# A hybrid decoder step: fewer VectorE instructions for GELU, gate and the samples' convolution, and the S5 recurrence in blocks

## The chip, the cores and the metric

The kernel runs on one core of one Trainium2 chip. The metric is the device time of one execution in microseconds, as the median of several runs. TensorE is called PE here, VectorE DVE, ScalarE ACT, GpSimd POOL, and SP is the engine that issues the DMAs.

## The reference

One inference step of two layers runs over a prompt of 16 + 512 tokens and over 8 samples of 8 tokens, with shared weights. Only layer 0 is touched by the change. It projects the input (width 2048) into five groups of 1024 columns and computes two branches:

```
h   = u_a * sigmoid(g_a)                                   # GLU
y_a = silu(LayerNorm(depthwise_conv31([state, h]) + b)) @ pw
x_t = a * x_(t-1) + B u_t      (64 groups, 64 complex states each)
y   = Re(C x) + D u_b
vg  = gelu(y) @ glu_w + glu_b;   y_b = v * sigmoid(gt)
mix = [y_a * silu(z_a), y_b * silu(z_b)];   out = mix @ w_out
x   = LayerNorm(ALPHA * x + out)
```

The samples start from given states (30 earlier rows of `h`, and the S5 state), the prompt from zeros. The states after the last token are outputs too.

## The kernel before

Activations lie channels on partitions, tokens along the free axis: 528 prompt columns and 8 x 8 sample columns, 592 in all (NP, NT). A projection is a list of jobs, one for each stripe of 128 output channels. A job takes the weights in pieces of four 128 x 128 blocks. Each piece is loaded by SP (`wraw`), rounded by ACT into `wh`, and DVE writes the remainder `wl = wraw - wh`. PE then runs 24 matmuls for it: three products (`wh` with both halves of the input, `wl` with the upper half), two column spans, four blocks. There are three `wraw`, two `wh` and two `wl` buffers, so a new `wh` waits for PE to finish an older piece.

Layer 0 (`layer0`) runs as several threads: loads, splits, matmuls, results of jobs, S5 tables, S5 application, convolution, normalisation. A planner (`Weave.run`) merges them at build time. It keeps an assumed clock for each engine, adds an assumed cost for each instruction (`cost`), and of the instructions that could start next takes the thread with the lowest number (splits first, convolution near the end). What comes out is one fixed order on each engine. On the chip each engine works through that order, and an instruction that waits holds all behind it. All these instructions carry the line of the planner's emission, L321, so they are told apart by tile names.

The parts in question: `glu_gate` and `glu` are two jobs for a stripe; the first turns `g_a` into a sigmoid in the tile `sg`, the second multiplies it into `hh`, a row of 862 columns (30 zeros, the prompt, then 8 samples of 30 + 8). `conv_taps` sums 31 shifted products of `hh` in the accumulator `taps`, which lies in PSUM: for each tap one DVE instruction on the prompt and one on the samples. The jobs function gives out stripe j's gate only when the taps of stripe j - 2 are all planned (`S.taps`), and gives out other jobs (inputs, `gates`) until then.

`s5_chain` runs on POOL, once for each half of the groups. It carries the chunk state through 66 chunks of 8 tokens in `s5xv`: product with the 2 x 2 form of a^8, sum of its two terms, sum into the next chunk. `s5_tables` and `s5_inject_tables` build matrices on POOL for PE, `s5_out` copies states to `s5xpad` on POOL, gathers PE's results in `s5y` and applies the GELU with `s5q`. `s5_setup` computes the powers of a once on DVE, at the start.

After the convolution the normalisation (`norms`) makes the input of the pointwise jobs (`pw`), `cbh` and `cbl`. The GELU results are loaded back and are the input of the `w_glu` jobs. Then `out_proj` follows, and layer 1, with code of their own.

Of the kernel before, what the change touches and what calls it, by code (L numbers as in the profile page):

```python
# [11 lines left out]
F32 = mybir.dt.float32  # L12
F32R = mybir.dt.float32r
I32 = mybir.dt.int32
# [561 lines left out]
def s5_setup(K, pool, S):  # L576
# [13 lines left out]
    dt, mag, th = t_("dt"), t_("mag"), t_("th")  # L590
    tmp = t_("ean"), t_("ear"), t_("eae", sh, I32)
# [5 lines left out]
    n = t_("n")  # L597
# [8 lines left out]
    sn, cs = t_("sn"), t_("cs")  # L606
# [11 lines left out]
    t1, t2 = t_("t1"), t_("t2")  # L618
# [38 lines left out]
    S.a8 = t_("a8", [128, 2, 2, 32])  # L657
# [3 lines left out]
    yield V.tensor_copy(S.a8[:, 0, 1], S.npi[:, :, 8])  # L661
    S.cr, S.ci = t_("cr", b3), t_("ci", b3)
# [124 lines left out]
def s5_out(K, pool, S, j, tables, u, yb, ahead):  # L787
# [43 lines left out]
def conv_taps(K, P, j, h, c, acc):  # L831


    cw = P["convw"][:, 31 * j:31 * j + 31]
    b8 = lambda z: z.rearrange("p (b t) -> p b t", b=8)
    hs = b8(h[:, 558:])
    for k in range(31):
        for sl, cut, src in ((slice(0, NP), lambda z: z, h[:, k:k + NP]), (slice(NP, NT), b8, hs[:, :, k:k + 8])):
            o = cut((c if k == 30 else acc)[:, sl])
            if k == 0:  # L840
                yield K.V.tensor_scalar(o, src, cw[:, 0:1], P["convb"][:, j:j + 1], op0=OP.mult, op1=OP.add)
            else:
                yield K.V.scalar_tensor_tensor(o, src, cw[:, k:k + 1], cut(acc[:, sl]), op0=OP.mult, op1=OP.add)


def layer0(K, O):
# [3 lines left out]
    with mk("l0") as p0:  # L850
# [3 lines left out]
        with banks(K, sps=2), mk("ln0") as pl, mk("cc", 8) as pc, mk("zs") as pz, ExitStack() as mid, \  # L854
# [50 lines left out]

            def glu_gate(j):
# [1416 lines left out]
```

## Time and profile before

| | us |
|---|---|
| median of 3 runs | 2764.46 |
| lowest and highest | 2763.84, 2769.56 |
| the profiled execution | 2762.25 |
| its span, first to last instruction | 2760.5 |
| PE, DVE, ACT, POOL busy in it | 2624.8, 1692.7, 1065.4, 963.7 |

An engine's busy time is the time in which it ran at least one instruction. The table of stretches gives this time for pieces of the span, with the clock that TensorE was granted there as a share of full speed. The list of waits gives the idle time of an engine just before an instruction, put down to whichever releaser came last. Busy time that lies beside a busier engine costs nothing by itself.

### The profile page before, as it was taken

How to read it: one execution, taken by the hardware profiler on the slowest of the kernel's cores; microseconds unless marked ns; L12 is line 12 of the kernel's file. 1: busy time of each engine (PE TensorE's matmuls, PEld its weight loads, DVE VectorE, ACT ScalarE, POOL GpSimd, SP SyncE). 2: the span in 40 equal slices, each digit the busy share in tenths (PEclk: the TensorE clock that was granted, in tenths of full speed). 3: DMA queues.
4: the chain of work that ended last, by engine and by line, in shares of the span. 5: the costliest groups of instructions: out<-in, count | busy, mean ns of one | idle time of the engine just before them, and what ended most of it. 6: DMA issues, size and time to landing. Idle time of an engine off the chain costs nothing. (4 is left out here: it accounts for less than half of the span.)

```text
span 2760.5 us, 49648 instructions
## 1 busy us (share of the span) xinstructions
PE 2624.8 (95%) x18848; PEld 2530.0 (92%) x18848; DVE 1692.7 (61%) x3282; ACT 1065.4 (39%) x2291; POOL 963.7 (35%) x1776
## 2 busy tenths in 40 slices
PE   8998899899999998999999999999999999999996
PEld 8998899899999998998888998998999989898996
DVE  7679798873443357666767667667563444446337
ACT  4322322252222234544545445455333334334223
POOL 1885677510002223244244253245200212212533
PEclk9999999999999999999999999999999999999998
DMA  6333343444333333212222222222333423425333
GB/s 197 94 98 90 99 103 87 98 129 135 114 101 111 104 117 113 85 61 79 71 67 77 75 77 69 65 78 68 100 105 88 138 91 124 140 86 169 115 110 103
DMA packets 202095, 278.33 MB, mean 101 GB/s; under 512 B 66808, under 2 KB 86008, under 8 KB 201856
## 3 DMA queue, kind: packets, MB, share of 16 engines
q1 hardware_dynamic: 199552, 270.30, 32.6%
q10 hardware_dynamic: 2304, 4.85, 0.5%
q8 instruction: 148, 2.42, 0.4%
q14 instruction: 91, 0.75, 0.1%
HBM read 232.54 MB, written 42.53 MB: 100 GB/s over the span
## 5 line engine op out<-in xcount | busy, mean ns | idle before, releaser
L321 PE MATMUL acc<-xh,wl 128*128 128x296 f32 (+2 forms) x3488 | 801.4, 306 | 38.2 <-DVE wl L321 38.2
L321 PE MATMUL acc<-xh,wh 128*128 128x296 f32 (+1 forms) x3520 | 806.2, 306 | 11.4 <-ACT xh L321 6.3
L321 PE MATMUL acc<-xl,wh 128*128 128x296 f32 (+1 forms) x3520 | 806.5, 305 | 0.0
L321 PEld LDWEIGHTS acc<-xh,wl 128*128 128x128 f32 x3488 | 573.9, 191 | 55.0 <-DVE wl L321 47.3
L321 DVE TENSOR_TENSOR wl<-wraw,wh 128x512 fp32r<-128x512 f32 x492 | 375.5, 763 | 381.3 <-ACT wh L321 359.1
L321 PEld LDWEIGHTS acc<-xh,wh 128*128 128x128 f32 x3520 | 582.3, 191 | 18.3 <-ACT xh L321 6.3
L321 PEld LDWEIGHTS acc<-xl,wh 128*128 128x128 f32 x3520 | 582.0, 191 | 5.7 <-issue 2.3
L321 ACT CAST wh<-wraw 128x512 fp32r<-128x512 f32 (+1 forms) x496 | 306.0, 618 | 713.7 <-PE acc L321 629.3
L321 DVE SCALAR_TENSOR_TENSOR taps<-hh,par,taps 128x528 f32<-128x528 f32 x464 | 245.7, 530 | 13.0
L490 PE MATMUL acc<-xh,wh 128*128 128x296 f32 (+2 forms) x832 | 182.1, 299 | 0.0
L490 PE MATMUL acc<-xh,wl 128*128 128x296 f32 (+1 forms) x832 | 180.8, 298 | 0.7 <-DVE wl L434 0.5
L490 PE MATMUL acc<-xl,wh 128*128 128x296 f32 (+2 forms) x832 | 180.5, 297 | 0.0
L433 ACT CAST wh<-wraw 128x512 fp32r<-128x512 f32 x100 | 62.0, 620 | 209.9 <-PE acc L490 207.2
L490 PEld LDWEIGHTS acc<-xh,wl 128*128 128x128 f32 x832 | 131.5, 188 | 1.5 <-DVE wl L434 1.4
L490 PEld LDWEIGHTS acc<-xh,wh 128*128 128x128 f32 x832 | 132.1, 189 | 0.5 <-ACT wh L433 0.2
L490 PEld LDWEIGHTS acc<-xl,wh 128*128 128x128 f32 x832 | 131.9, 188 | 0.4
L434 DVE TENSOR_TENSOR wl<-wraw,wh 128x512 fp32r<-128x512 f32 x100 | 70.0, 701 | 95.9 <-ACT wh L433 90.3
L321 POOL TENSOR_TENSOR rnt<-rcf,rn 128x75 f32<-128x75 f32 (+14 forms) x240 | 87.1, 363 | 84.0 <-DMA rcf<-rcd 67.7
L1155 POOL TENSOR_TENSOR rr<-rr,lna 128x592 f32<-128x592 f32 (+1 forms) x2 | 3.5, 1736 | 309.9 <-ACT lna L404 309.9
L404 POOL TENSOR_TENSOR lnb<-lnb,rr 128x592 f32<-128x592 f32 (+1 forms) x24 | 42.5, 1770 | 186.1 <-DVE rr L1124 186.1
L321 ACT ACT_TABLE_LOAD x71 | 91.1, 1283 | 16.9 <-DVE rh L321 15.0
L321 POOL TENSOR_TENSOR k<-mc,mch 128x512 fp32r<-128x512 f32 x32 | 42.1, 1315 | 157.3 <-ACT mch L321 133.0
(577 smaller groups left out, 4812.4 us busy)
## 6 DMA issues: line engine op xcount, KB each, us to landing
wraw<-w_e SPq DMA_DIRECT2D x160, 256.0 KB, 3.3
wraw<-w_m SPq DMA_DIRECT2D x160, 256.0 KB, 3.0
wraw<-w_r SPq DMA_DIRECT2D x132, 256.0 KB, 3.0
wraw<-w_eo SPq DMA_DIRECT2D x64, 256.0 KB, 2.9
wraw<-w_oo SPq DMA_DIRECT2D x64, 256.0 KB, 3.0
rcf<-rcd SPq DMA_DIRECT2D x16, 640.0 KB
wraw<-w_glu SPq DMA_DIRECT2D x32, 256.0 KB, 2.6
mc<-mc SPq DMA_DIRECT2D x32, 256.0 KB, 3.1
```

Source lines behind the costliest of these rows:

```text
L321: getattr(eng.e, fn)(out, *a, **kw)
L404: getattr(eng.e, fn)(out, *a, **kw)
L433: K.nc.scalar.copy(H, x)
L434: (e or K.nc.vector).tensor_tensor(L, x, H.bitcast(F32), op=OP.subtract)
L490: K.nc.tensor.matmul(o, w[:, kk], x[:, a:b], start=st, stop=sp)
L1155: G.tensor_tensor(r, r, N.c, op=OP.subtract)
```

## The change

Three parts, all in layer 0.

GELU and gate: the scale 0.044715 goes into ACT's square, so that one three-operand instruction forms the argument of tanh, and GELU's factor 0.5 goes into the `w_glu` weights. The gate's tanh is written by ACT straight into `hh`, one three-operand instruction multiplies (tanh + 1) by `u_a`, and the factor 0.5 goes into the weights of the `glu` jobs. Jobs marked `half` halve the weights while splitting them. The tile `sg` is gone; `hh` is allocated, zeroed at its head and given the sample state in the gate's job instead of in the `glu` job.

Convolution of the samples: for two samples at a time, POOL multiplies all 31 shifted windows by the taps in one instruction (2 x 8 x 31 elements), and DVE sums over the 31 with one `tensor_reduce`, placed five taps later. ACT adds the bias. The prompt's taps stay as they were.

S5 recurrence: the 66 chunks are cut into 11 blocks of 6. Five steps advance all 11 blocks at once, ten steps of the old kind carry the last state from block to block, and five steps add the carried state, times powers of a^8, to the chunks inside. The powers are made in the setup. The scratch tile is that of the setup's temporaries.

The diff, cut to its core (`out` and `out_gate` become `half` jobs too):

```diff
+    S.scratch = t_("tmp", [128, 32 * S5B])
+    dt, mag, th, ean, ear, eae, n, sn, cs, t1, t2 = (S.scratch[:, 32 * i:32 * i + 32] for i in range(11))
+    tmp = ean, ear, eae.bitcast(I32)
...
+    S.aa = t_("aa", [128, S5K, 2, 2, 32])
+    S.a8 = S.aa[:, 0]
     yield V.tensor_copy(S.a8[:, 0, 0], S.pr[:, :, 8])
     yield V.tensor_copy(S.a8[:, 1, 1], S.pr[:, :, 8])
     yield V.tensor_copy(S.a8[:, 1, 0], S.pi[:, :, 8])
     yield V.tensor_copy(S.a8[:, 0, 1], S.npi[:, :, 8])
+    m4 = [128, 2, 2, 32]
+    m = pool.tile(m4, F32, name="s5am", tag="s5tt", bufs=1)
+    for k in range(1, S5K):
+        for i, o in enumerate((S.aa[:, k], m)):
+            yield tt(o, bc(S.a8[:, :, i, None, :], m4), bc(S.aa[:, k - 1, None, i], m4), OP.mult)
+        yield tt(S.aa[:, k], S.aa[:, k], m, OP.add)
...
+S5K, S5B = 6, 11
 def s5_chain(K, pool, S, hf, out):
     G = K.G
     xv = S.xv
-    a8 = S.a8[:, :, :, 16 * hf:16 * hf + 16]
+    aa = S.aa[:, :, :, :, 16 * hf:16 * hf + 16]
+    a8 = aa[:, 0]
+    xb = xv[:, :, :, 1:67].rearrange("p r g (b k) -> p r g b k", k=S5K)
+    def add(dst, src, k, n):
+        sh = [128, 2, 16, n]
+        t = S.scratch[:, :32 * n].rearrange("p (o g b) -> p o g b", o=2, b=n)
+        for r in range(2):
+            yield G.tensor_tensor(t, bc(aa[:, k, :, r, :, None], sh), bc(src[:, r, None], sh), op=OP.mult)
+            yield G.tensor_tensor(dst, dst, t, op=OP.add)
+    for k in range(1, S5K):
+        yield from add(xb[:, :, :, :, k], xb[:, :, :, :, k - 1], 0, S5B)
     sh = [128, 2, 2, 16]
-    for c in range(66):
-        t = pool.tile(sh, F32, name="s5c1", bufs=1)
-        q = pool.tile([128, 2, 16], F32, name="s5c2", bufs=1)
-        yield G.tensor_tensor(t, a8, bc(xv[:, None, :, :, c], sh), op=OP.mult)
-        yield G.tensor_tensor(q, t[:, :, 0], t[:, :, 1], op=OP.add)
-        yield G.tensor_tensor(xv[:, :, :, c + 1], xv[:, :, :, c + 1], q, op=OP.add)
+    for b in range(1, S5B):
+        t = pool.tile(sh, F32, name="s5c4", bufs=1)
+        x, y = xb[:, :, :, b, S5K - 1], xb[:, :, :, b - 1, S5K - 1]
+        yield G.tensor_tensor(t, aa[:, S5K - 1], bc(y[:, None], sh), op=OP.mult)
+        yield G.tensor_tensor(t[:, :, 0], t[:, :, 0], t[:, :, 1], op=OP.add)
+        yield G.tensor_tensor(x, x, t[:, :, 0], op=OP.add)
+    for k in range(S5K - 1):
+        yield from add(xb[:, :, :, 1:, k], xb[:, :, :, :S5B - 1, S5K - 1], k, S5B - 1)
...
-    yield A.square(q, y)
-    yield V.tensor_scalar(q, q, 0.044715, 1.0, op0=OP.mult, op1=OP.add)
-    yield V.tensor_tensor(q, q, y, op=OP.mult)
+    yield A.activation(q, y, AF.Square, scale=math.sqrt(0.044715))
+    yield V.scalar_tensor_tensor(q, q, 1.0, y, op0=OP.add, op1=OP.mult)
     yield A.activation(q, q, AF.Tanh, scale=math.sqrt(2.0 / math.pi))
-    yield V.tensor_scalar(y, y, 0.5, None, op0=OP.mult)
     yield V.scalar_tensor_tensor(y, q, 1.0, y, op0=OP.add, op1=OP.mult)
...
+def windows(z):
+    part_, (sb, nb), (st, _) = z.ap
+    return AP(z.tensor, z.offset, [part_, [sb, nb], [st, 8], [st, 31]])
+def conv_taps(K, P, pool, j, h, c, acc):
+    V, G = K.V, K.G
+    cw, b = P["convw"][:, 31 * j:31 * j + 31], P["convb"][:, j:j + 1]
+    hs = h[:, 558:].rearrange("p (b t) -> p b t", b=8)
+    sh = [128, 2, 8, 31]
+    acc = acc[:, 0:NP]
     for k in range(31):
-        for sl, cut, src in ((slice(0, NP), lambda z: z, h[:, k:k + NP]), (slice(NP, NT), b8, hs[:, :, k:k + 8])):
-            o = cut((c if k == 30 else acc)[:, sl])
-            if k == 0:
-                yield K.V.tensor_scalar(o, src, cw[:, 0:1], P["convb"][:, j:j + 1], op0=OP.mult, op1=OP.add)
-            else:
-                yield K.V.scalar_tensor_tensor(o, src, cw[:, k:k + 1], cut(acc[:, sl]), op0=OP.mult, op1=OP.add)
+        src = h[:, k:k + NP]
+        if k % 8 == 0:
+            i = k // 4
+            z = pool.tile(sh, F32, name="win", bufs=1)
+            yield G.tensor_tensor(z, windows(hs[:, i:i + 2]), bc(cw[:, None, None, :], sh), op=OP.mult)
+        if k == 0:
+            yield V.tensor_scalar(acc, src, cw[:, 0:1], b, op0=OP.mult, op1=OP.add)
+        else:
+            yield V.scalar_tensor_tensor(c[:, 0:NP] if k == 30 else acc, src, cw[:, k:k + 1], acc, op0=OP.mult, op1=OP.add)
+        if k % 8 == 5:
+            yield V.tensor_reduce(c[:, NP + 8 * i:NP + 8 * i + 16].rearrange("p (b t) -> p b t", b=2), z, axis=AX.X, op=OP.add)
+    yield K.A.activation(c[:, NP:NT], c[:, NP:NT], AF.Identity, bias=b)
...
+            def parts(h, acc):
+                return ((h[:, 30:326], acc[0]), (h[:, 326:558], acc[1][:, 0:232]),
+                        (b8(h[:, 558:])[:, :, 30:38], b8(acc[1][:, 232:296])))
             def glu_gate(j):
                 def then(acc):
-                    g = cv.tile([128, NT], F32, name="sg")
-                    for p, (a, b) in zip(acc, SPAN0):
-                        yield A.activation(g[:, a:b], p, AF.Tanh, scale=0.5)
-                    w.give("acc", "acc")
-                    yield V.tensor_scalar(g, g, 0.5, 0.5, op0=OP.mult, op1=OP.add)
-                    SG.append(g)
-                return Job(I["w_e"], 8 + j, SPAN0, then)
-            def glu(j):
-                b8 = lambda z: z.rearrange("p (b t) -> p b t", b=8)
-                def then(acc):
-                    g = SG.popleft()
                     h = cv.tile([128, 862], F32, name="hh", bufs=2)
                     hs = b8(h[:, 558:])
+                    yield G.memset(h[:, 0:30], 0.0)
                     yield D.dma_start(hs[:, :, 0:30], I["sconv"][j])
-                    yield G.memset(h[:, 0:30], 0.0)
-                    yield V.tensor_tensor(h[:, 30:326], g[:, 0:296], acc[0], op=OP.mult)
-                    yield V.tensor_tensor(h[:, 326:558], g[:, 296:NP], acc[1][:, 0:232], op=OP.mult)
-                    yield V.tensor_tensor(hs[:, :, 30:38], b8(g[:, NP:NT]), b8(acc[1][:, 232:296]), op=OP.mult)
+                    for o, p in parts(h, acc):
+                        yield A.activation(o, p, AF.Tanh, scale=0.5)
+                    w.give("acc", "acc")
+                    SG.append(h)
+                return Job(I["w_e"], 8 + j, SPAN0, then)
+            def glu(j):
+                def then(acc):
+                    h = SG.popleft()
+                    hs = b8(h[:, 558:])
+                    for o, p in parts(h, acc):
+                        yield V.scalar_tensor_tensor(o, o, 1.0, p, op0=OP.add, op1=OP.mult)
                     w.give("acc", "acc")
                     H.append(h)
                     rows = slice(128 * j, 128 * j + 128)
                     yield D.dma_start(O["o_conv"][rows, 0, :], h[:, 528:558])
                     yield D.dma_start(O["o_conv"][rows, 1:9, :], hs[:, :, 8:38])
-                return Job(I["w_e"], j, SPAN0, then)
+                return Job(I["w_e"], j, SPAN0, then, half=True)
...
+            elif job.half:
+                yield w.A.mul(wh, raw, 0.5)
+                yield w.V.scalar_tensor_tensor(wl, raw, 0.5, wh.bitcast(F32), op0=OP.mult, op1=OP.subtract)
             else:
                 yield w.A.copy(wh, raw)
                 yield w.V.tensor_tensor(wl, raw, wh.bitcast(F32), op=OP.subtract)
```

## Rows read from the trace of the kernel before

**Rows 1.** Page, part 1: engine, busy us (share of the span), instructions
```profile
PE 2624.8 (95%) x18848; PEld 2530.0 (92%) x18848; DVE 1692.7 (61%) x3282; ACT 1065.4 (39%) x2291; POOL 963.7 (35%) x1776
```

**Rows 2.** Stretches of layer 0: us, then each engine's busy us (instructions), PEclk, DMA
```profile
120.00:180.00 60.00, 54.55 (x385) 52.58 (x386) 57.42 (x109) 13.12 (x25) 47.82 (x135) 1.00 0.34 92
180.00:220.00 40.00, 38.34 (x274) 37.17 (x274) 22.65 (x43) 8.21 (x15) 30.58 (x76) 1.00 0.32 96
220.00:320.00 100.00, 84.49 (x593) 82.49 (x592) 96.78 (x154) 25.48 (x49) 54.22 (x72) 0.93 0.35 89
360.00:420.00 60.00, 54.58 (x389) 52.46 (x387) 57.56 (x110) 12.87 (x24) 48.38 (x118) 1.00 0.40 102
...
440.00:480.00 40.00, 38.05 (x274) 36.76 (x273) 38.48 (x72) 9.52 (x18) 29.51 (x76) 1.00 0.29 85
480.00:540.00 60.00, 50.70 (x341) 49.74 (x340) 53.70 (x90) 12.97 (x25) 31.97 (x49) 0.89 0.43 102
...
600.00:660.00 60.00, 60.00 (x441) 60.00 (x441) 30.14 (x44) 24.39 (x39) 0.00 (x0) 1.00 0.46 126
```

**Rows 3.** Waits, 0 to 820 us: engine and tile, releaser, us, times, longest
```profile
PE acc L321 <- DVE wl L321: 38.2, 34, 5.1
...
PE acc L321 <- ACT xh L321: 6.3, 1, 6.3
...
DVE taps L321 <- POOL hh L321: 7.7, 2, 4.2
```

**Rows 4.** VectorE by line and form, 0 to 820: busy us, mean ns, idle
```profile
L321 DVE SCALAR_TENSOR_TENSOR taps<-hh,par,taps 128x528 f32<-128x528 f32 x232 | 179.1, 772 | 7.4
L321 DVE TENSOR_TENSOR wl<-wraw,wh 128x512 fp32r<-128x512 f32 x207 | 164.8, 796 | 154.4 <-ACT wh L321 149.9 <-DMA s5ul<-ub 4.4
L321 DVE SCALAR_TENSOR_TENSOR taps<-hh,par,taps 128x64 f32<-128x64 f32 x232 | 66.6, 287 | 5.7
L321 DVE TENSOR_TENSOR s5q<-s5q,s5y 128x592 f32<-128x592 f32 x8 | 23.0, 2875 | 0.1
...
L321 DVE TENSOR_SCALAR s5y<-s5y 128x592 f32<-128x592 f32 x8 | 9.3, 1161 | 0.1
L321 DVE TENSOR_SCALAR s5q<-s5q 128x592 f32<-128x592 f32 x8 | 7.5, 943 | 5.0 <-ACT s5q L321 5.0
L321 DVE SCALAR_TENSOR_TENSOR s5y<-s5q,s5y 128x592 f32<-128x592 f32 x8 | 7.4, 931 | 0.1
...
L321 DVE TENSOR_SCALAR sg<-sg 128x592 f32<-128x592 f32 x8 | 5.1, 640 | 1.2 <-ACT sg L321 1.2
```

**Rows 5.** GpSimd by line and form, 0 to 820 us
```profile
L321 POOL TENSOR_TENSOR s5c<-s5a,s5xv 128x64 f32<-128x64 f32 x132 | 51.0, 386 | 9.2
L321 POOL TENSOR_TENSOR s5xv<-s5xv,s5c 128x32 f32<-128x32 f32 x132 | 45.2, 342 | 9.5
L321 POOL TENSOR_TENSOR s5c<-s5c 128x32 f32<-128x32 f32 x132 | 42.9, 325 | 9.3
...
L321 POOL TENSOR_TENSOR s5c<-s5a,s5xv 128x256 f32<-128x256 f32 x4 | 2.6, 646 | 0.1
...
L321 POOL TENSOR_TENSOR s5wa<-s5rr,k 128x512 f32<-128x512 f32 x8 | 9.3, 1161 | 54.6 <-DVE k L321 51.6 <-PE sps L321 3.0
...
L321 POOL TENSOR_TENSOR s5wa<-s5wa,s5t 128x512 f32<-128x512 f32 x8 | 11.8, 1472 | 0.5
```

**Rows 6.** VectorE by line and form, 60 to 100 us
```profile
L321 DVE TENSOR_TENSOR wl<-wraw,wh 128x512 fp32r<-128x512 f32 x9 | 10.5, 1163 | 24.8 <-ACT wh L321 24.8
```

**Rows 7.** Timeline around 256 us: start, us, what [idle before, releaser]
```profile
255.78 4.68 DVE L321 TENSOR_TENSOR s5q<-s5q,s5y 128x592 f32<-128x592 f32 x1
...
261.33 0.86 PE L321 MATMUL acc<-xh,wl 128*128 128x296 f32 x2 [5.12 <-DVE wl L321]
```

**Rows 8.** Instructions that read the convolution's split result: ns min/median/max, first and last start
```profile
L321 ACT CAST cbh<-cc x16: 687/996/1333, 569.9 to 641.5; 128x592 fp32r<-128x592 f32 x16
...
L321 PE MATMUL acc<-cbh,wh x384: 295/298/307, 670.5 to 827.0; 128*128 128x296 f32 x192
```

More of the change, by code (lines that the diff above doesn't have):

```diff
@@ L617, in s5_setup @@
     yield V.memset(S.pi[:, :, 0], 0.0)
-    t1, t2 = t_("t1"), t_("t2")
     for k in range(2, 9):
@@ L904, in inputs @@
                 return Job(I["w_e"], 24 + j, SPAN0, then, tag=tag, after=after)
+            b8 = lambda z: z.rearrange("p (b t) -> p b t", b=8)
+            def parts(h, acc):
+                return ((h[:, 30:326], acc[0]), (h[:, 326:558], acc[1][:, 0:232]),
+                        (b8(h[:, 558:])[:, :, 30:38], b8(acc[1][:, 232:296])))
             def glu_gate(j):
                 def then(acc):
-                    g = cv.tile([128, NT], F32, name="sg")
-                    for p, (a, b) in zip(acc, SPAN0):
-                        yield A.activation(g[:, a:b], p, AF.Tanh, scale=0.5)
+                    h = cv.tile([128, 862], F32, name="hh", bufs=2)
+                    hs = b8(h[:, 558:])
+                    yield G.memset(h[:, 0:30], 0.0)
+                    yield D.dma_start(hs[:, :, 0:30], I["sconv"][j])
+                    for o, p in parts(h, acc):
+                        yield A.activation(o, p, AF.Tanh, scale=0.5)
                     w.give("acc", "acc")
-                    yield V.tensor_scalar(g, g, 0.5, 0.5, op0=OP.mult, op1=OP.add)
-                    SG.append(g)
+                    SG.append(h)
                 return Job(I["w_e"], 8 + j, SPAN0, then)
             def glu(j):
-                b8 = lambda z: z.rearrange("p (b t) -> p b t", b=8)
                 def then(acc):
-                    g = SG.popleft()
-                    h = cv.tile([128, 862], F32, name="hh", bufs=2)
+                    h = SG.popleft()
                     hs = b8(h[:, 558:])
-                    yield D.dma_start(hs[:, :, 0:30], I["sconv"][j])
-                    yield G.memset(h[:, 0:30], 0.0)
-                    yield V.tensor_tensor(h[:, 30:326], g[:, 0:296], acc[0], op=OP.mult)
-                    yield V.tensor_tensor(h[:, 326:558], g[:, 296:NP], acc[1][:, 0:232], op=OP.mult)
-                    yield V.tensor_tensor(hs[:, :, 30:38], b8(g[:, NP:NT]), b8(acc[1][:, 232:296]), op=OP.mult)
+                    for o, p in parts(h, acc):
+                        yield V.scalar_tensor_tensor(o, o, 1.0, p, op0=OP.add, op1=OP.mult)
                     w.give("acc", "acc")
@@ L964, in then @@
                     w.give("acc", "acc")
-                return Job(I["w_glu"], j, SPAN0, then, X=Y)
+                return Job(I["w_glu"], j, SPAN0, then, X=Y, half=True)
             def out_gate(j):
@@ L975, in then @@
                     yield from mixed(z)
-                return Job(I["w_glu"], 8 + j, SPAN0, then, X=Y)
+                return Job(I["w_glu"], 8 + j, SPAN0, then, X=Y, half=True)
             def jobs():
@@ L1040, in convs @@
                     c = pc.tile([128, NT], F32, name="cc")
-                    yield from conv_taps(K, P, j, H[j], c, taps)
+                    yield from conv_taps(K, P, cv, j, H[j], c, taps)
                     S.taps += 1
@@ L1216, with __init__ @@
 class Job:
-    def __init__(self, W, s, spans, then, paired=False, final=False, X=None, tag="acc", after=None):
+    def __init__(self, W, s, spans, then, paired=False, final=False, X=None, tag="acc", after=None,
+                 half=False):
         self.W, self.s, self.spans, self.then, self.paired, self.final = W, s, spans, then, paired, final
-        self.after = after
+        self.after, self.half = after, half
         self.X, self.tag, self.nk = X, tag, W.shape[2] if W is not None else 0
```

8 lines of the change are left out of this document (removed).

## The prediction

> **What bounds the kernel now.** I read the engines' shares first. TensorE (PE) is busy 95% of the span [rows 1], so the change, which touches only VectorE (DVE), GpSimd (POOL) and ScalarE (ACT) work of layer 0, can gain only what PE loses there. The table of stretches comes next: the reader is to see PE at 60.00 of 60 us from 600 us on, with DVE half idle, and PE short of full before that, wherever DVE stands at 90% or more [rows 2]. Third, the list of waits over layer 0 says who ends PE's idle time: DVE's split of a weight piece (`wl`), 38.2 us in 34 waits, the longest 5.1; the other large one, 6.3 us, is the start of the kernel [rows 3]. So layer 0's front is bounded by PE where DVE has room, and by DVE where the taps of the convolution and the GELU fill its queue, because the one `wl` that PE needs stands in that queue behind them.
>
> Three kinds of stretch follow [rows 2]. (a) Taps without GELU, 120 to 180, 360 to 420 and 440 to 480 us: PE idles 5.45 + 5.42 + 1.95 = 12.8 of 160 us, 8%. (b) Taps with GELU, 220 to 320 and 480 to 540 us: 15.5 + 9.3 = 24.8 of 160 us, 15.5%, and here alone the granted clock falls to 0.93 and 0.89, that is 7.0 + 6.6 = 13.6 us of work lost at the lower level (1.2 GHz of 2.4). (c) DVE light, 180 to 220 us: DVE 22.65 of 40, PE still idles 1.7, 4%. In all about 51 us can be called into question: 12.8 + 24.8 + 13.6.
>
> **What the change takes from and gives to DVE.** *Convolution.* A tap of the prompt costs 0.772 us, one of the samples 0.287 us for 64 elements, each with a gap of some 0.024 us (5.7 us before 232) [rows 4]. 248 sample taps go (8 stripes of 31): 248 x 0.311 = 77 us. 32 sums of 496 elements come. No such sum is in the trace; the two tap rows give 1.045 ns an element ((772 - 287)/464), so 0.287 + 432 x 0.001045 = 0.74 us, 32 x 0.76 = 24 us. Bounds: 0.54 us an instruction (the `sg` scaling ran 592 elements in 0.640 [rows 4]) and twice my value if its access pattern halves the rate, 18 to 48 us. Net 53 us off, bounds 29 to 59. *GELU.* The two scalings go: 7.5 + 9.3 = 16.8 us. The product `s5q` (2.875 us mean) becomes a three-operand form with the same two SBUF inputs, and the last step stays (0.931) [rows 4]. I take 2.875 as unchanged; if it ran as its three-operand neighbour does, another 15.6 us would go. *Gate.* Eight `sg` scalings go, 5.1 us [rows 4]; the products keep size and inputs. *Weights.* 64 pieces (8 `glu`, 16 `w_glu` jobs) are halved as they are split: ACT scales instead of casting, DVE uses the three-operand form on the same 512 elements. Both at nothing; the cover is ACT's and DVE's room, half of them after 670 us where PE has none idle. A 0.1 us longer DVE form would cost 6 us of DVE, less than 2 of PE. *Setup.* 15 small products of 128 elements for the powers of the matrix, at the 0.287 row 4.3 us on DVE, early; POOL, which waits for the setup, starts its tables that much later.
>
> **POOL.** Before, a half of the recurrence is 66 steps of three dependent instructions, 0.386 + 0.325 + 0.342 plus gaps of 0.07: 1.26 us, 83 us a half [rows 5]. After, there are 20 instructions on 352 elements, 20 on 320 and 10 steps of the old three. Between the rows at 256 (0.646) and 512 elements (1.161) lies 2.0 ns an element: 0.84 and 0.78 us; with gaps 20 x 0.91 + 20 x 0.85 + 10 x 1.26 = 48 us. That is 35 us less a half, 70 in all. Against it come 32 products of 496 elements; the tables' instructions on 512 took 1.161 and 1.472 us [rows 5], so 37 to 47 us. POOL ends some 28 us lighter, but its instructions are longer.
>
> That matters for the `wl` splits. Beside the tables of 512 elements, between 60 and 100 us with DVE otherwise nearly idle, `wl` takes 1.163 us [rows 6]; over the whole of layer 0 it is 0.796 [rows 4]. The clearest case is the stretch around 256 us: one `s5q` product took 4.68 us while POOL ran product after product, and PE stood 5.12 us for the `wl` behind it [rows 7]. The sample taps that the change removes had one input in PSUM and ran at their 0.287 us all the same. The stretches (a) and (b) hold 1982 matmuls [rows 2], 24 to a piece, so some 83 `wl`. I add 0.35 us to a third of them: 10 us, bounds 0 and 0.37 x 83 = 31 us.
>
> The Trainium skill (SBUF — State Buffer, "Who interferes with whom") says that a DVE instruction with two SBUF inputs and a GpSimd one that reads SBUF share a port pair that the first takes for its whole instruction, the other blocking fully, and that `tensor_reduce` on this chip never contends. The trace agrees that the two exclude each other, but 4.68 us is longer than one POOL instruction and one product, so DVE did not get in at the first change of owner. By the rule alone `s5q` would be at most its own 0.8 behind one instruction of 1.2, 2.0 us, and DVE would save 7 us more than in my sum.
>
> Net on DVE: 53 + 16.8 + 5.1 - 4.3 - 10 = 61 us, of the 320 us of (a) and (b).
>
> **From DVE to PE.** The convolutions are fed by the jobs, so DVE will still be filled while one runs, only for fewer microseconds: 61 of 320 is 19%. (a) The 160 us shrink to 130, and the idle share falls between the 8% of (a) and the 4% of (c); I take 6%: 7.8 us remain of 12.8, gain 5.0. (b) The blocks ahead of a `wl` fall from scaling plus product (0.94 + 2.88) to the product alone, and 1.16 + 0.93 to 0.93. The product's own long block remains. I take 14 of 24.8 us, gain 10.8; bounds 0 (the product blocks as before) and 18 (4% on 160 us). Clock: its falls lie in the stretches with the long gaps; I take half back, 6.8, bounds 0 and 13.6. The gate's `memset` moves a job ahead, so DVE's 7.7 us on `hh` [rows 3] go; to PE that is worth 1.
>
> **Waits added.** Each sum on DVE waits for a product on POOL that is issued some five taps ahead: 5 x 0.8 plus one or two `wl` makes 5 us, against 1.2 us for the product and about 1 for the instruction ahead of it. Behind the waiting sum stand taps and `wl`, and PE behind that. The next product in turn waits for the sum (one buffer), with the recurrence queued behind it. I take 2 us; bounds 0 and 20. The sample state's load moves from the `glu` job to its gate, so on SP's queue it passes the four weight loads of that job; it waits for a buffer that two stripes earlier filled, whose taps the job order has already demanded. Free, unless it waits: then weight loads stand behind it. The recurrence's end and the normalisation are covered: their first operand is ready at 569.9 us, PE takes it at 670.5 [rows 8], 100 us of other jobs.
>
> Sum: 5.0 + 10.8 + 6.8 + 1 - 2 = 21.6 us. The profiled execution took 2762.25 us (span 2760.5 and 1.75 around it), so 2740.7 there; the median of the runs, 2764.46, stands 2.2 us above it, so **2743 us** as a median. With every bound good, (a) gives 6.4 (4% on 160 us), (b) 18, the clock 13.6 and `hh` 1: 39 us. With every bound bad the waits' 20 us outweigh what (a) gives.
>
> **Rivals.**
> *DVE stops being a bound.* If the product `s5q` and the tap ends fall so that `wl` is never late by more than in (c), PE idles 4% of 320 us, 12.8 instead of 37.6, and the clock stays up: 24.8 + 13.6 = 38 us, 2726 us, down to 2713 if the rate is that of 600 us on, none at all. For it: 180 to 220 us runs at that rate with POOL at 76% [rows 2]. Against: taps still fill DVE when a stripe is ready.
> *POOL's longer instructions eat it.* If most `wl` cost the upper 0.37 us more and the product blocks as before, (b) and the clock keep their loss and only (a) and `hh` gain, 6 us less the 2 of the waits: 2760 us, no difference. For it: 1.163 us beside the tables, and the 4.68. Against: the stretches with dense POOL products are those of the tables, which don't change. The page of the Trainium skill named above (SBUF — State Buffer) speaks for this rival, since work moves from instructions that touch one SBUF input to POOL.
> *Slower: DVE waits for POOL's products.* POOL is late for its 32 products by more than the margin of 5 - 2.2 = 2.8 us plus some 1.4 us that a piece of weights (24 matmuls at 60/441 us, 3.3 us [rows 2]) leaves beside its split of 0.8 and an ACT cast taken as long. Each further microsecond idles PE; from 0.85 us a product on (27 us in all) the gain is gone and a loss of over 5 us begins. At 1.1 us: 35 - 21.6 = 13 us slower, 2778. For it: an in-order queue and a wait in each direction for every product, and DVE waited up to 4.2 us for a POOL `memset` [rows 3]. Against: only two of eight `memset`s made DVE wait.
> The change not doing what it says is no separate case: the instructions are written out; it would be the second.
>
> **How the numbers follow.** Forecast 2743, chance 0.54; DVE unbound 2726, 0.25; eaten 2760, 0.13; slower 2778, 0.08. A measurement of this kernel tells about 0.2%, 5.5 us, from no change. Faster 0.54 + 0.25 = 0.79, same 0.13, slower 0.08. The range leaves out the slower case and the best end of the second: 2714 to 2764.
>
> **What would show it.** Sample taps gone, 32 sums near 0.74 us, 32 POOL products near 1.2; a half of the recurrence near 48 us; `s5q` still above 2 us; PE's waits for `wl` near 20 us instead of 38.2, clock above 0.95 in every stretch. It is wrong if `wl` means rise past 1 us, if DVE's waits for the products pass 20 us, or if PE's loss moves to another wait.

## The result and the profile after

| kernel | median, us | runs | ratio to before, 95% interval |
|---|---|---|---|
| before | 2766.74 (2763.84 to 2769.56) | 4 | |
| after | 2734.43 (2729.48 to 2739.83) | 4 | 0.9884 [0.9860, 0.9907] |

The change makes the kernel 32 us faster, 1.2%. The profiled executions give 2762.25 and 2733.02 us, 29.2 us less. The page's first part, engines with busy time and share, answers [rows 1]:

```profile
PE 2619.6 (96%) x18848; PEld 2530.1 (93%) x18848; DVE 1658.4 (61%) x3057; ACT 1066.7 (39%) x2305; POOL 982.1 (36%) x1552
```

PE does the same work in a shorter span; all of the gain is time that it had lost. The stretches of layer 0 in the kernel after, with the columns of [rows 2] (us, then busy us of PE, PE's weight loads, DVE, ACT and POOL, each with its instructions, clock, DMA share, GB/s):

```profile
120.00:180.00 60.00, 56.77 (x399) 55.61 (x398) 44.66 (x52) 14.26 (x28) 53.57 (x75) 0.97 0.44 108
180.00:220.00 40.00, 39.63 (x290) 39.08 (x288) 39.36 (x53) 9.63 (x18) 35.84 (x39) 1.00 0.34 95
220.00:320.00 100.00, 92.36 (x675) 91.22 (x674) 75.80 (x85) 29.73 (x58) 68.08 (x85) 0.97 0.41 105
...
360.00:420.00 60.00, 59.39 (x436) 58.90 (x435) 46.43 (x61) 13.54 (x26) 56.87 (x77) 1.00 0.43 106
...
440.00:480.00 40.00, 38.84 (x294) 38.42 (x293) 29.42 (x39) 12.38 (x25) 30.37 (x46) 1.00 0.38 108
480.00:540.00 60.00, 54.23 (x381) 53.27 (x380) 46.93 (x63) 13.89 (x27) 22.00 (x36) 0.94 0.46 116
...
600.00:660.00 60.00, 60.00 (x442) 60.00 (x441) 29.71 (x46) 24.07 (x38) 0.00 (x0) 1.00 0.53 146
```

The reader is to see DVE: it stood at 89 to 97% in (a) and (b) before, and now stands at 74 to 78% there. PE idles 3.2 + 0.6 + 1.2 = 5.0 us in (a), where it was 12.8, and 7.6 + 5.8 = 13.4 in (b), where it was 24.8. The clock's loss is 1.8 + 3.0 + 3.6 = 8.4 us, where it was 13.6. The stretches are the same times in both kernels, not quite the same work, since the kernel after is some microseconds ahead in them. Over the first 600 us, before and after:

```profile
0.00:600.00 600.00, 548.13 (x3912) 535.59 (x3913) 485.60 (x898) 183.57 (x334) 367.44 (x688) 0.98 0.41 110
```

```profile
0.00:600.00 600.00, 571.00 (x4137) 563.47 (x4138) 461.46 (x689) 192.99 (x363) 384.87 (x464) 0.99 0.43 116
```

PE's idle time falls from 51.9 to 29.0 us; with the clock's 5.2 that makes 28.1 of the profile's 29.2 us. DVE is busy 24 us less there (485.6 to 461.5), but PE, and the work with it, is further ahead in the same 600 us. Over the whole span, which holds all of each kernel's work, DVE is busy 34.3 us less (1692.7 to 1658.4), not 61. The instructions of VectorE from 0 to 820 us (form, count, busy us, mean ns, idle before) say why, beside [rows 4]:

```profile
L321 DVE SCALAR_TENSOR_TENSOR taps<-hh,par,taps 128x528 f32<-128x528 f32 x232 | 178.4, 769 | 5.0
L321 DVE TENSOR_TENSOR wl<-wraw,wh 128x512 fp32r<-128x512 f32 x146 | 145.9, 1000 | 92.2 <-ACT wh L321 85.9 <-PE acc L321 3.2 <-DMA cc<-yb 2.6
L321 DVE SCALAR_TENSOR_TENSOR wl<-wraw,wh 128x512 fp32r<-128x512 f32 x64 | 55.5, 867 | 62.9 <-ACT wh L321 56.7 <-DMA s5ul<-ub 3.5 <-PE acc L321 2.7
L321 DVE TENSOR_REDUCE cc<-win 128x16 f32<-128x496 f32 x32 | 21.2, 661 | 0.0
L321 DVE SCALAR_TENSOR_TENSOR s5y<-s5q,s5y 128x592 f32<-128x592 f32 x8 | 19.8, 2476 | 1.0 <-ACT s5q L321 1.0
...
L321 DVE SCALAR_TENSOR_TENSOR s5q<-s5q,s5y 128x592 f32<-128x592 f32 x8 | 6.9, 862 | 11.7 <-ACT s5q L321 11.7
```

The sample taps are gone and the sums cost little. But the 210 `wl` take 145.9 + 55.5 = 201.4 us, 0.96 each, where 207 took 164.8, and of GELU's two products it is now the second (`s5y`) that is held up, 2.48 us instead of 0.93, while the first fell from 2.88 to 0.86. GpSimd, beside [rows 5]:

```profile
L321 POOL TENSOR_TENSOR win<-hh,par 128x496 f32<-128x496 f32 x32 | 42.0, 1314 | 67.1 <-DVE cc L321 65.4 <-DMA s5ul<-ub 1.6
...
L321 POOL TENSOR_TENSOR s5xv<-s5xv,s5tmp 128x352 f32<-128x352 f32 x20 | 24.3, 1214 | 0.3
L321 POOL TENSOR_TENSOR s5tmp<-s5aa,s5xv 128x352 f32<-128x352 f32 x20 | 23.2, 1158 | 0.3
L321 POOL TENSOR_TENSOR s5xv<-s5xv,s5tmp 128x320 f32<-128x320 f32 x20 | 22.9, 1144 | 1.2
L321 POOL TENSOR_TENSOR s5tmp<-s5aa,s5xv 128x320 f32<-128x320 f32 x20 | 21.2, 1059 | 0.9
```

The waits (who, for whom, us in total, times, longest), beside [rows 3]:

```profile
POOL win L321 <- DVE cc L321: 65.4, 13, 14.9
...
PE acc L321 <- DVE wl L321: 18.4, 14, 3.7
```

For the experiments one more mark is of use, the start of the last pointwise matmul on `cbh`, with which layer 0's front ends (min/median/max ns, first and last start in us). It was 827.0 us before [rows 8]:

```profile
L321 PE MATMUL acc<-cbh,wh x384: 295/298/307, 639.8 to 796.3; 128*128 128x296 f32 x192
```

The mark is 30.7 us earlier: the whole gain arises ahead of it.

### The profile page after: what moved, and what is told of

It reads as the page before. It is cut to its first block, busy times and chain, and to the rows that moved or that the text cites. A ratio compares the mean times of both kernels' runs of the same rounds, so it can differ in the third digit from the quotient of the medians.

```text
span 2731.2 us, 49197 instructions
## 1 busy us (share of the span) xinstructions
PE 2619.6 (96%) x18848; PEld 2530.1 (93%) x18848; DVE 1658.4 (61%) x3057; ACT 1066.7 (39%) x2305; POOL 982.1 (36%) x1552
## 5 line engine op out<-in xcount | busy, mean ns | idle before, releaser
L321 PE MATMUL acc<-xh,wl 128*128 128x296 f32 (+2 forms) x3488 | 799.9, 306 | 18.7 <-DVE wl L321 18.4
L321 DVE TENSOR_TENSOR wl<-wraw,wh 128x512 fp32r<-128x512 f32 x428 | 354.5, 829 | 315.0 <-ACT wh L321 294.0
L321 ACT CAST wh<-wraw 128x512 fp32r<-128x512 f32 x432 | 266.4, 617 | 584.7 <-PE acc L321 526.1
L321 DVE SCALAR_TENSOR_TENSOR taps<-hh,par,taps 128x528 f32<-128x528 f32 x232 | 178.4, 769 | 5.0
L433 ACT CAST wh<-wraw 128x512 fp32r<-128x512 f32 x100 | 62.0, 620 | 208.1 <-PE acc L490 204.0
L434 DVE TENSOR_TENSOR wl<-wraw,wh 128x512 fp32r<-128x512 f32 x100 | 70.1, 702 | 93.0 <-ACT wh L433 87.4
```

Of the source, the lines that this page charges most:

```text
L321: getattr(eng.e, fn)(out, *a, **kw)
L433: K.nc.scalar.copy(H, x)
L434: (e or K.nc.vector).tensor_tensor(L, x, H.bitcast(F32), op=OP.subtract)
```

## The experiments

Two explanations stood against each other once the result was known. **A**, the prediction's own: PE gains because DVE has less to do. **B**, formed from the two traces: PE gains because the order written for DVE fits what DVE can do. The planner's formula for most DVE instructions of n elements is 0.07 + n/960 us, and 0.06 more with a column operand. That makes 0.68 us for a tap of the prompt and 0.20 for one of the samples; the trace has 0.772 and 0.287, and 0.024 between two [rows 4]. So in the kernel before every pair of taps takes some 0.23 us longer than the plan has it. **C** was the rival on the other side: POOL's instructions hold up DVE.

In the kernel after the misfit of the taps is smaller still than the formula alone says. A tap of the prompt takes 0.11 us longer than its 0.68. But the planner also keeps a DVE instruction 0.13 us away from one whose result it reads (`SAME` in the kernel), and each tap reads the sum that the tap before it wrote. In the kernel before the sample's tap filled that time. In the kernel after, two taps in a row lie 0.68 + 0.13 = 0.81 us apart in the plan, and 0.79 (0.769 and 0.022 between) in the trace. Only where another instruction stands between two taps are the 0.11 us left.

The kernels tried, with the kernel after once more. Layer 0's mark is the start of the last pointwise matmul in the profile; it was 827.0 us in the kernel before.

| kernel | ratio to before, 95% interval | median of before beside it, and its own, us | layer 0's mark, us |
|---|---|---|---|
| after | 0.9884 [0.9860, 0.9907] | 2766.74, 2734.43 | 796.3 |
| conv_alone | 0.9869 [0.9849, 0.9889] | 2767.47, 2729.01 | 792.3 |
| gelu_alone | 0.9923 [0.9905, 0.9941] | 2767.47, 2745.27 | 807.5 |
| s5_alone | 1.0043 [1.0029, 1.0057] | 2767.47, 2780.44 | 841.4 |
| order_v_018 | 0.9866 [0.9846, 0.9886] | 2767.47, 2728.27 | 794.9 |
| conv_gelu | 0.9881 [0.9867, 0.9895] | 2762.51, 2729.26 | 799.5 |
| order_conv_gelu | 0.9882 [0.9867, 0.9897] | 2762.51, 2731.24 | 796.7 |
| order_s5 | 0.9925 [0.9912, 0.9939] | 2762.51, 2741.63 | 811.9 |
| s5_serial | 1.0028 [1.0019, 1.0038] | 2762.51, 2770.88 | 839.0 |
| order_taps64 | 0.9916 [0.9899, 0.9932] | 2768.46, 2748.41 | 806.0 |
| conv_short_order | 1.0112 [1.0096, 1.0127] | 2768.46, 2802.13 | 833.3 |
| order_conv | 0.9898 [0.9883, 0.9913] | 2768.46, 2741.34 | 807.9 |
| after_no_products | 0.9877 [0.9861, 0.9893] | 2768.46, 2735.91 | 795.8 |

The planner also writes the order of layer 1. A kernel whose cost formula was changed for all of DVE (order_v_018, order_conv_gelu, order_s5, order_conv, conv_short_order) therefore runs layer 1 in another order too, and only layer 0's mark is read for these.

### The parts one by one

**conv_alone.** The hunks of `conv_taps` alone, of which the call is shown:

```diff
...
-                    yield from conv_taps(K, P, j, H[j], c, taps)
+                    yield from conv_taps(K, P, cv, j, H[j], c, taps)
```

> Only the samples' convolution is changed (POOL products, DVE sums); GELU, gate and recurrence are those of before. Theory A, PE gains in step with the microseconds taken from DVE in the full stretches: this part had 53 of my 61 us, so it alone gives most of the 32 us, 20 to 30 us faster than before. Theory B, PE gains because DVE stops falling behind the written order (a sample tap is planned at 0.20 us and takes 0.29 plus a gap): also 20 to 30 us, with the regular small waits for wl (0.3 to 0.6 us) gone and the long ones beside the GELU left. Rival C, POOL's products cost what the taps gave: under 8 us faster.

It gained 38 us at the median, 1.3%, as much as the whole change. A and B both expected a gain, of 20 to 30 us, so this run doesn't tell them apart. PE's waits for a `wl` fell from 34 to 11:

```profile
PE acc L321 <- DVE wl L321: 19.1, 11, 4.2
```

**gelu_alone.** The hunks of `s5_out`, `glu_gate`, `glu` and the `half` jobs alone, of which two lines of the GELU are shown:

```diff
...
-    yield V.tensor_scalar(q, q, 0.044715, 1.0, op0=OP.mult, op1=OP.add)
-    yield V.tensor_tensor(q, q, y, op=OP.mult)
+    yield V.scalar_tensor_tensor(q, q, 1.0, y, op0=OP.add, op1=OP.mult)
...
```

> Only GELU and gate are changed. Theory A: 16.8 + 5.1 = 22 us less DVE work, about 7 to 10 us faster. Theory B: the long waits beside the GELU shrink only by the removed scalings, 3 to 8 us faster. Rival D, the two-input instruction of the GELU simply waits for POOL in another place: within 3 us of before.

22 us faster, well beyond every one of the expectations. DVE's two products of the GELU in this kernel:

```profile
L321 DVE SCALAR_TENSOR_TENSOR s5y<-s5q,s5y 128x592 f32<-128x592 f32 x8 | 10.8, 1348 | 1.1 <-ACT s5q L321 1.1
L321 DVE SCALAR_TENSOR_TENSOR s5q<-s5q,s5y 128x592 f32<-128x592 f32 x8 | 9.2, 1149 | 17.3 <-ACT s5q L321 17.3
```

A and B had expected 3 to 10. `s5q` takes 1.15 us here, and the longest wait of PE for a `wl` falls from 5.1 to 2.6:

```profile
PE acc L321 <- DVE wl L321: 21.9, 29, 2.6
```

In conv_alone, where the GELU is untouched, its old two-operand form takes 1.04:

```profile
L321 DVE TENSOR_TENSOR s5q<-s5q,s5y 128x592 f32<-128x592 f32 x8 | 8.3, 1036 | 0.1
```

So the 2.88 us of [rows 4], and the long stops of PE behind it, belong less to the instruction than to where the order of the kernel before puts it beside POOL. In every other kernel of the table it is shorter than 2.88, 0.86 to 1.72. A shorter `s5q` isn't enough for a gain, though: s5_alone and s5_serial below have it at 1.43 and 1.64 us and are slower than the kernel before. And since the taps are costed here as before, this gain is neither that of B's misfit nor, at 22 us, of A's size.

**s5_alone.** The hunks of `s5_setup` and `s5_chain` alone, of which the new loop's head is shown:

```diff
...
-    for c in range(66):
+    for k in range(1, S5K):
+        yield from add(xb[:, :, :, :, k], xb[:, :, :, :, k - 1], 0, S5B)
...
```

> Only the recurrence is changed: 48 to 56 us of POOL a half instead of 83, longer instructions, 4 us more DVE in the setup. Theories A and B: POOL was not a bound, so within 4 us of before. Rival C, the longer POOL instructions hold up DVE's two-input instructions: 5 to 15 us slower than before, wl mean in 120 to 180 us above 0.95 instead of 0.79. Rival E, a shorter recurrence is itself a gain: over 5 us faster.

12 to 13 us slower: C, by the time expected; A and B had no more than 4 us either way. C's sign, a mean `wl` above 0.95 us from 120 to 180 us, came too (1.45), but through a single one of 14; the mean of the others is 0.86. The timeline around 117 us (start, length, engine, what; in brackets the idle time before) shows the most of it:

```profile
115.47 1.13 POOL L321 TENSOR_TENSOR s5xv<-s5xv,s5tmp 128x352 f32<-128x352 f32 x1
...
116.56 1.40 POOL L321 TENSOR_TENSOR s5ca<-s5ca,s5t 128x576 f32<-128x576 f32 x1
...
117.03 9.04 DVE L321 TENSOR_TENSOR wl<-wraw,wh 128x512 fp32r<-128x512 f32 x1
117.92 0.96 POOL L321 TENSOR_TENSOR s5tmp<-s5aa,s5xv 128x352 f32<-128x352 f32 x1
118.85 1.15 POOL L321 TENSOR_TENSOR s5cb<-s5cr,s5npi 128x576 f32<-128x576 f32 x1
119.97 1.09 POOL L321 TENSOR_TENSOR s5xv<-s5xv,s5tmp 128x352 f32<-128x352 f32 x1
121.02 1.15 POOL L321 TENSOR_TENSOR s5t<-s5ci,k 128x576 f32<-128x576 f32 x1
122.14 0.97 POOL L321 TENSOR_TENSOR s5tmp<-s5aa,s5xv 128x352 f32<-128x352 f32 x1
123.08 1.39 POOL L321 TENSOR_TENSOR s5cb<-s5cb,s5t 128x576 f32<-128x576 f32 x1
124.44 1.09 POOL L321 TENSOR_TENSOR s5xv<-s5xv,s5tmp 128x352 f32<-128x352 f32 x1
125.47 0.51 POOL L321 MEMSET s5bd<- 128x512 f32 x1
...
126.13 0.86 PE L321 MATMUL acc<-xh,wl 128*128 128x296 f32 x2 [8.91 <-DVE wl L321]
```

A `wl` of 0.69 us takes 9.04. POOL alternates between the table's products (`s5ca`, `s5t`, `s5cb`) and the recurrence's (`s5tmp`, `s5xv`), each starting as the one before it ends. Here DVE got in only when POOL came to a `memset`, which reads nothing: the `wl` ends 0.60 us after the `memset` starts. PE stands 8.9 us for it. The second half of the recurrence has the same, a `wl` of 8.74 us with PE idle for 10.2.

**s5_serial.** The tables of the output wait until the recurrence of their half is done, by this line and a counter behind `s5_chain`, which now starts ahead of the table:

```diff
-                    yield lambda: S.applied >= n - 1
+                    yield lambda: S.applied >= n - 1 and S.chained >= k * (1 + n // 8)
```

> The recurrence in blocks alone, order costs as before, but the tables of the output are built only after the recurrence of their half, so that POOL never has two independent chains of long instructions to alternate between. Theory C in its sharp form (DVE's two-input instruction gets in only when POOL pauses, and two interleaved chains leave no pause for 9 us): the stalls of 8.9 and 10.2 us go and the time falls by 8 to 20 us against s5_alone, to within 6 us of before. If the length of the single POOL instruction is what costs, or the 4 us of setup on DVE: the time stays within 4 us of s5_alone.

The two long stops are gone; the longest wait of PE for a `wl` is 5.5 us:

```profile
PE acc L321 <- DVE wl L321: 50.2, 33, 5.5
```

But the sum of these waits stays at 50 us (53.3 in s5_alone), in more and shorter pieces, and the time falls by some 4 us only, within the intervals and short of the 8 to 20 that C in its sharp form had. The alternation explains the two stops, not the cost of the recurrence in blocks. How much of that cost is the length of POOL's instructions and how much the changed order, these runs don't settle.

### The order by itself

**order_v_018.** One number in the planner's formula, with every instruction of the kernel before kept:

```diff
-    return 0.07 + n / (1920 if fast else 960) + 0.06 * cols
+    return 0.18 + n / (1920 if fast else 960) + 0.06 * cols
```

> The kernel before with the same instructions, but the planner that writes the order takes each DVE instruction 0.11 us longer (a fixed part of 0.18 instead of 0.07 us, nearer to the taps in the trace). Theory A: DVE's work is the same, so within 4 us of before. Theory B: DVE's order no longer runs ahead of what it can do, wl stands where PE needs it, 10 to 25 us faster than before without one instruction less; fewer taps stand between two wl and the convolution ends later.

37 us faster, more than the 10 to 25 of B; 32.1 of it lie ahead of layer 0's mark. The first 600 us:

```profile
0.00:600.00 600.00, 572.58 (x4147) 566.35 (x4148) 490.43 (x893) 179.22 (x335) 370.72 (x688) 0.98 0.42 114
```

DVE is busy 490.4 us there, 5 us more than before, and PE 572.6, 24 more. So less DVE work isn't needed for a gain of this size. The timeline of DVE shows what changed. Take each `wl` with all that DVE runs behind it up to the next one, idle time left out, from 100 to 560 us. Such a block exceeds PE's 3.3 us for a piece 69 times in 102 in the kernel before, 40 in 110 in this one, 43 in 113 in conv_alone and 54 in 110 in the kernel after; the longest is 14.7, 9.5, 10.2 and 9.4 us. The count agrees with B but doesn't rank the kernels: gelu_alone has 65 in 108, and gains.

**order_taps64.** The longer cost for the samples' taps alone:

```diff
-    return 0.07 + n / (1920 if fast else 960) + 0.06 * cols
+    small = n == 64 and out.space == PSUM
+    return (0.18 if small else 0.07) + n / (1920 if fast else 960) + 0.06 * cols
```

> The kernel before, same instructions; the planner takes only the samples' taps (64 elements, 0.29 us in the trace, 0.20 in the planner's formula) 0.11 us longer. Theory B: half of the planner's shortfall on a pair of taps is here (0.11 of 0.23 us), so a third to two thirds of the 37 us of order_v_018, 12 to 25 us faster than before. Theory A: within 4 us of before.

20 us faster at the median, 21.0 at layer 0's mark: two thirds of what order_v_018 has there, at the upper end of what B expected. This is the cleanest of the order's runs, since 240 of DVE's costs are all that differs (the samples' taps that write PSUM) and layer 1 is left alone. Part of it is again `s5q`, 1.02 us instead of 2.88; how much of the gain is the taps' excess and how much that the GELU no longer meets POOL is not settled, but both are the order's.

**conv_short_order.** The convolution part, with a plan in which DVE's instructions are too short again:

```diff
-    return 0.07 + n / (1920 if fast else 960) + 0.06 * cols
+    return -0.045 + n / (1920 if fast else 960) + 0.06 * cols
```

> The convolution part alone, but the planner takes each DVE instruction 0.115 us shorter, so that a tap is as short in the plan of this kernel as a pair was in the kernel before (0.23 us too short a tap). Theory B, the convolution's gain came from the order: most of its 36 us goes, 0 to 15 us faster than before. Theory A, it came from the 56 us of work taken from DVE: 28 us faster or more remain.

Layer 0's mark is 833.3, 41 us later than in conv_alone and 6.3 later than before, though the part's instructions are all there. The total is worse still: behind the mark, where the same formula orders layer 1, the profiled execution takes some 26 us longer than that of conv_alone. The edit isn't quite what the expectation says. With the planner's 0.13 us between dependent instructions two taps in a row lie 0.695 us apart in this plan, 0.10 and not 0.23 less than in the trace; and all other DVE instructions, `wl` among them, are costed short too. In the first 600 us, and in two stretches:

```profile
0.00:600.00 600.00, 547.71 (x3871) 534.94 (x3872) 422.10 (x656) 171.31 (x325) 407.33 (x720) 0.97 0.40 107
```

```profile
20.00:120.00 100.00, 90.72 (x645) 89.77 (x645) 49.98 (x136) 35.71 (x70) 58.21 (x68) 0.93 0.44 123
...
220.00:320.00 100.00, 89.61 (x640) 88.07 (x640) 76.81 (x97) 26.05 (x51) 65.24 (x89) 0.93 0.40 99
```

DVE is busy 422 us, 64 us less than in the kernel before, and PE 547.7, the same as before. Not all of the loss belongs to the taps: between 20 and 120 us, where the small instructions of the setup are costed too short as well, 9.3 us idle and 7 us of clock are lost, 15 us more than in conv_alone. From 120 to 690 us, idle and clock together, the kernel before loses 57 us, conv_alone 27 and this one 51. So of the part's 30 us there, 7 are left. Its longest block, counted as above, is 15.9 us. With the two runs above this speaks against A as the whole account: DVE's order gives the gain without less work, and less work in a bad order hardly gives any. That the taps alone carry it isn't shown by this run, since the costs of all DVE instructions were changed.

### What stands in the way of more

**conv_gelu**, the hunks of conv_alone and gelu_alone together, without the recurrence:

> Convolution and GELU/gate are changed, the recurrence is that of before. If the recurrence in blocks costs time through its long POOL instructions (theory C), this is faster than the whole change by 6 to 15 us, so 2715 to 2728 us. If the recurrence helps or is nothing beside the other two parts, it equals the whole change, 2734, or is slower. The two parts alone gave 36 and 21 us; since PE lost only some 60 us in this stage, they can't add fully.

Equal to the whole change by the ratio, and 3 us later at the mark: the second case of the expectation. The recurrence that costs 12 us alone costs nothing here. One wait may be a reason in its favour. POOL, with the old recurrence and the new products, is 7.1 us late for the normalisation, and no more than 2.1 in any other kernel:

```profile
PE sps L321 <- POOL lnb L321: 7.1, 1, 7.1
```

**order_conv_gelu**, **order_conv** and **order_s5** are conv_gelu, conv_alone and s5_alone with the one edit of order_v_018:

> Convolution and GELU/gate changed, recurrence as before, and the planner takes each DVE instruction 0.11 us longer. Theory B, PE loses where DVE's order runs ahead of DVE: the two parts and the new order remove the same loss, so this is at most 10 us faster than conv_gelu. Theory A, work taken from DVE counts by itself: the gains of order (37 us) and parts (36 and 21) add, up to what PE lost, 2705 to 2712 us.

> The convolution part alone with the planner taking each DVE instruction 0.11 us longer, near the taps of the trace. If the two remove one and the same loss (theory B): within 8 us of each alone, 2722 to 2732 us. If they add: below 2715 us. This is also a candidate for a faster kernel than either of the two compared.

> Recurrence in blocks alone, with the order written for DVE instructions 0.11 us longer. Against order_v_018 (2728 us), which has the old recurrence: theory C, the POOL instructions stand in DVE's way whatever the order: 6 to 20 us slower. If s5_alone was slow only because of its order: within 4 us.

The gains don't add: order_conv_gelu is where the parts alone already were, as B expected. order_conv is worse than either alone (19.1 us at the mark against 32.1 and 34.7), which neither expected. There PE reaches the pointwise jobs at 627.7 us, earlier than in any other kernel, and then waits for their operands, which are cast from 610.7 us on:

```profile
L321 PE MATMUL acc<-cbh,wh x384: 295/299/615, 627.7 to 807.9; 128*128 128x296 f32 x192
...
L321 ACT CAST cbh<-cc x16: 684/957/1306, 610.7 to 666.2; 128x592 fp32r<-128x592 f32 x16
```

```profile
PE acc L321 <- ACT cbh L321: 13.8, 5, 3.2
...
PE acc L321 <- DVE wl L321: 8.0, 5, 3.8
```

The 100 us by which the normalisation was covered before [rows 8] are used up: PE is there 43 us earlier, and the convolution's result 41 us later (569.9 before). The bound has moved to the hand-over. The formula offers a reason that no run tests. A tap behind a tap is now planned at 0.79 + 0.13 = 0.92 us, more than the trace's 0.79, so the plan lets the convolution run slower than DVE could. order_s5 lies 17 us behind order_v_018 at the mark. It has 8.7 us of the wait for `cbh`, and one of 7.8 us for a `wl` that took 11.19 us beside ten POOL instructions of the two chains. So the recurrence in blocks costs time under another order as well, in part through C's mechanism.

**after_no_products**, the whole change with a fill in the place of POOL's products:

```diff
-            yield G.tensor_tensor(z, windows(hs[:, i:i + 2]), bc(cw[:, None, None, :], sh), op=OP.mult)
+            yield G.memset(z, 0.0)
```

> The whole change with the samples' 32 POOL products left out: a fill of the same tile stands in their place, which writes only, so the samples' convolution is not computed. Theory C, a POOL instruction that reads SBUF holds up DVE's two-input ones: the wl mean up to 690 us falls from 1.0 to 0.85 or less, and the kernel is 4 to 12 us faster than the whole change (2734). If the products stand in nobody's way: wl as before and within 3 us. A gain above 15 us would mean that the sums' waits for the products cost more than I saw.

No difference in time (0.9877 against 0.9884), and the `wl`, in both forms, take 0.98 us in the mean up to 690 us against 1.01. By the expectation the products stand in nobody's way, but the trace doesn't bear that out. The planner costs a fill at 0.45 us and a product at 1.24, so POOL's order changed with the edit, and at 114 us the two chains of s5_alone met. One `wl` took 12.97 us beside twelve POOL instructions, until a `memset`, and PE stood for 9.6:

```profile
114.35 12.97 DVE L321 SCALAR_TENSOR_TENSOR wl<-wraw,wh 128x512 fp32r<-128x512 f32 x1 [0.18 <-ACT wh L321]
```

```profile
PE acc L321 <- DVE wl L321: 21.8, 8, 9.6
```

In the kernel after PE's longest stop for a `wl` is 3.7 us. Without the long one the mean here is 0.91:

```profile
L321 DVE TENSOR_TENSOR wl<-wraw,wh 128x512 fp32r<-128x512 f32 x144 | 127.3, 884 | 80.7 <-ACT wh L321 75.0 <-PE acc L321 2.7 <-DMA cc<-yb 2.6
L321 DVE SCALAR_TENSOR_TENSOR wl<-wraw,wh 128x512 fp32r<-128x512 f32 x33 | 45.8, 1389 | 49.5 <-ACT wh L321 45.8 <-DMA s5ul<-ub 3.5
```

And in the kernel after the longest `wl` ran beside a product (`win`) that stands between two steps of the recurrence:

```profile
152.27 1.13 POOL L321 TENSOR_TENSOR s5xv<-s5xv,s5tmp 128x352 f32<-128x352 f32 x1
152.42 5.31 DVE L321 TENSOR_TENSOR wl<-wraw,wh 128x512 fp32r<-128x512 f32 x1 [2.58 <-ACT wh L321]
...
154.95 1.18 POOL L321 TENSOR_TENSOR win<-hh,par 128x496 f32<-128x496 f32 x1
156.09 1.09 POOL L321 TENSOR_TENSOR s5xv<-s5xv,s5tmp 128x352 f32<-128x352 f32 x1
```

So what the products cost DVE stays open: a gain by leaving them out may be hidden behind the new stop. The rival of DVE waiting for the products is out all the same, by the kernel after itself, whose sums waited 0.0 us.

No kernel tried is faster than the kernel after by more than the intervals: conv_alone and order_v_018 equal it, one with a third of its edits, the other with one number.

One rival of B isn't tested: that nearly any other order would have gained, because that of the kernel before happens to put `s5q` beside POOL. No order was changed but through the costs, and the longer fixed part was tried at one value only.

## Why the prediction was right, and where it was not

The forecast was 2743 us with a range of 2714 to 2764 and 0.79 for faster; 2734.4 was measured. The gain was 32 us where the sum had 21.6, midway between the forecast and the first rival, 2726. The time lies in the range, but in part by luck: the sum counts microseconds taken from DVE, and the runs put most of the gain on an order that the sum doesn't look at.

- **The bound** was read rightly: PE's loss was the waits for `wl`, and they fell from 38.2 to 18.4 us, against the 20 that the prediction named. All but some 1 us of the gain lies ahead of 600 us.
- **The terms of PE**: (a) was to keep 7.8 us and kept 5.0; (b) was to keep 14 and kept 13.4; the clock was to give back 6.8 and gave 5.2. The mis-sized terms are (a), 2.8 us more, and the time outside (a) and (b), where another 3.7 us went that the sum had left alone.
- **DVE's balance failed.** It was to have 61 us less work and has 34 less over the span. The sums (0.66 us for 0.74) and the products on POOL (1.31 us between 1.16 and 1.47) were sized well. The `wl` were not: 10 us were allowed for contention, and they took 34 us more (201.4 - 210 x 0.796). `s5q`, taken as unchanged at 2.88 us, fell to 0.86, and `s5y` rose to 2.48, so the two together took 26.7 us where they had taken 30.4.
- **POOL's balance failed too.** The 80 block instructions of the recurrence took 91.6 us, 1.15 each, where 0.81 was worked out from rows with less beside them. With the ten old steps a half takes some 60 us where 48 were expected, and POOL, which was to end 28 us lighter, is busy 18 us more.
- **The step from DVE to PE failed as a reason.** It said that DVE "will still be filled while one runs, only for fewer microseconds", and made PE's gain from those microseconds. order_v_018 has the gain without them and order_taps64 two thirds of it, and conv_short_order has them with hardly a gain. The runs put it on the order of DVE's instructions instead: a pair of taps took 0.23 us longer than the plan had it, and with the samples' taps that misfit left the plan. How much of the whole change's 32 us is this, and how much the GELU's new place beside POOL, isn't separated. The prediction saw that one `wl` stands behind the taps, but not that the number of taps between two of them is the planner's choice, made from a formula that [rows 4] contradicts.
- **Waits added**: 2 us were taken, and none came by the products. The sums waited 0.0 us; POOL waited instead, 65.4 us for DVE to free the one buffer, while PE's waits for POOL came to 0.5 us. The move of `hh` to the gate's job freed DVE of its 7.7 us, as worked out.
- **Rivals.** "DVE stops being a bound" came as near as the forecast: PE kept 18.4 us idle in (a) and (b), between the forecast's 21.8 and this rival's 12.8. "Eaten" had a part of its mechanism, a dearer `wl` (0.96 us for 0.80, where it named up to 0.37 more), and the gain came all the same. "Slower" didn't have its mechanism, since DVE waited for no product. s5_alone is 12 us slower, with DVE twice held up by POOL for some 9 us, but how much of the 12 is that isn't settled; in the whole change this cost doesn't show beside the two other parts.
- **Signs.** PE's waits for `wl` (18.4 us for 20) and the sums came as forecast. `s5q` above 2 us didn't come, nor a clock above 0.95 in every stretch (0.94 from 480 to 540 us). And one sign of being wrong did: the mean of `wl` passed 1 us, at 1.01 up to 690 us, while PE gained.

The port pair of the Trainium skill (SBUF — State Buffer, "Who interferes with whom") bears on this. That a sum never contends agrees with the rows: 0.66 us in each of the kernels that have it. That an instruction which only writes doesn't block a two-input one agrees with the `wl` that gets in at the `memset`. That whoever issues first holds the pair for its whole instruction doesn't account for the wait of 9.04 us: the `wl` waited through eight instructions of POOL, not one.

## What to carry to other kernels

Where an order is written ahead of time from assumed costs, set these costs beside the trace before taking work away: here one constant was worth as much as three rewritten stages, and one rewritten stage won 30 us between 120 and 690 us, or 7, with the order around it. Price an edit at the engine that bounds the stage, by how often that engine is made to wait, not by the microseconds taken from the engine beside it. And try the parts alone: one of three here costs time by itself, and one gives the whole gain.

## What the runs showed of the hardware

A DVE instruction with two SBUF inputs can be held up far longer than one POOL instruction. A `wl` of 0.69 us became 9.04 in s5_alone and 12.97 in after_no_products while POOL ran two independent chains without a pause, and both ended 0.6 us after POOL had started a `memset`. The cost of such an instruction in a profile therefore says as much of what POOL was given at that moment as of the instruction: the same two-operand `s5q` took 2.88 us in the mean in the kernel before, 1.04 in conv_alone and 1.02 in order_taps64.
